# First mixer of a two-layer transformer step: VectorE's modulation sums from three tiles in the heads and four in the out-projection, tied to the attention's reciprocals, at other rates

## The chip, the cores and the metric

One core of one Trainium2 chip. The metric is the device time of one execution in microseconds (us). The instructions run on TensorE (PE: matmuls, with its weight loads PEld beside them), VectorE (DVE), ScalarE (ACT), GpSimd (POOL), and SyncE (SP), whose queue issues nearly all DMA transfers. Each engine runs its own list of instructions in a fixed order, and waits on semaphores for what others produce.

## The reference, cut to what matters

One inference step of a network of width D = 2048 with two layers, for 128 context tokens and 128 latent tokens. Each layer is a mixer (attention) and a gated feed-forward part with a convolution; each of these reads a normalized input that is shifted and scaled, and adds its output times a gate:

```python
mod = silu(cond) @ w_ada            # per layer 6 x 2048 numbers for each of the two groups
shift, scale, gate = ...            # of the mixer, and three more of the feed-forward part
h = rmsnorm(x, g) * (1 + scale) + shift
x = x + gate * mixer(h)             # layer 0: MLA and GQA heads, one in- and one out-projection
h = rmsnorm(x, g2) * (1 + scale2) + shift2
x = x + gate2 * ffn(h)              # layer 1 the same with differential attention
```

The matrix `w_ada` is read once, and each of its blocks of 128 x 2048 numbers gives only two columns of `mod`: it is memory traffic with little arithmetic. All of it is float32.

## The kernel before, in words

The kernel holds the activations in SBUF with the features on the partitions: a tile is 128 features by 256 tokens (128 context, 128 latent). A product of a weight block and an activation is made of three TensorE matmuls on numbers split in two: weight high times activation high (`wh`, `hx`), `wh` times the activation's low part, and weight low (`wl`) times the high part. A weight tile `raw` of 1 MB comes by DMA (line 284); ScalarE casts it to `wh` and VectorE subtracts to get `wl` (line 258 and 259, in pieces of 128 x 1024, or 128 x 512 where `fine[0]` is set). TensorE's order within a stage is: the gemms of the stage one after the other (16 blocks of 128 x 128 each, 48 matmuls of 128 x 256).

The stages of the first layer, by the profile's times: the in-projection to some 200 us, the attention heads to 316 us (`mixer_ab`, loop over `h`), the out-projection to 421 us (`out_ab`, loop over `c`, sixteen output blocks, each with its residual sum `x` on line 878), then the normalization of the feed-forward's input and the feed-forward itself.

`w_ada` for the later parts is worked off beside these stages in two ways:

- On TensorE: `row_step` loads a tile `araw` of 1 MB (line 615, two buffers), multiplies it with the condition (`ada<-araw,condw`, in pairs of tiles), ScalarE copies the sums (`am`, line 447), and TensorE transposes them (line 113) for VectorE to add up (lines 455 to 464). `pump(rate)` after a gemm gives so many steps of it; what is left over of a unit lies in the list `later`.
- On VectorE: class `Deep`. A tile of 512 KB (`block`, `kvb` or `more`, line 553) is multiplied with the condition of the two groups and summed along its rows, two instructions of 128 x 1024 (line 543, each with a short read of the accumulator). `deep.rate` says how many such sums a pump issues; `deep.tiles` names the homes that the tiles take turns in, `deep.junk` the scratch that the products go to; with `deep.ahead` the next tile is loaded when one is begun. `settle()` at `h == 6` finishes what was loaded in the heads, `flush()` in the out-projection issues all the steps that are left. In the first layer it has 64 sums in all.

The order on each engine is that of a scheduler in the framework, which is free to move instructions by its own costs, except those given to `keep_order`, which stay in program order among themselves. VectorE's modulation sums and their loads are so pinned; TensorE's instructions are when `pe.in_turn` is set. SP's queue is one list too: a load that waits for its buffer holds up those behind it.

The out-projection begins with `first_three`, which runs blocks c = 0 to 2 together, since the last heads come late; from c = 3 on it is one gemm after the other. A gemm there begins with the second half of its weight tile (`first=8`).

Of the kernel before, what the change touches and what calls it, by code (L numbers as in the profile page):

```python
# [18 lines left out]
P = 128  # L19
D = 2048  # L20
KD = D // P
T = 128
NT = 2 * T
# [33 lines left out]
QUIET = [4, 3, 3]  # L57
# [28 lines left out]
RLIMIT = {"ab": 16, "ffn0": 17, "c": 22, "ffn1": 22}  # L86
FLIMIT = {"ab": 0, "ffn0": 12, "c": 12, "ffn1": 16}

SIDE = {"in3": 0.5, "heads": 1.9, "out0": 1.85, "c": 2.2, "outc": 2.0}
UW = NT + 2  # L90
INV = {2048: 0, 768: 1, 512: 2, 128: 3, 256: 4}

# [2 lines left out]
def step_kernel(ctx: ExitStack, tc: tile.TileContext, A: dict):  # L95
# [298 lines left out]
    pinned = [False]  # L394
    done = set()
    later = []

    class HalfUnit:

# [38 lines left out]
    def ada_finish(l, j, q):  # L438

        got = {}  # L440

        def home():
            return T_(ppool["ada"], [P, 512], "ada", bufs=1)

        def copy():
            got["am"] = T_(tmp, [P, 512], "am", bufs=1)
            (keep_order if pe.in_turn else lambda i: i)(act.copy(got["am"], ada["ps"]))

        def turn(pin=None):
            pt = bank() if pin else home()  # L450
            pin = pin or (lambda i: i)
            for b in range(4):
                pin(pe.transpose(pt[:, b * P:(b + 1) * P], got["am"][:, b * P:(b + 1) * P], ident))
            out = mod[:, l, j, 4 * q:4 * q + 4]
            dve.tensor_reduce(out=out, in_=pt.rearrange("p (b g r) -> p b r g", b=4, g=4)[:, :, 0:2],
                              axis=AX.X, op=ALU.add)
            dve.tensor_tensor(out=out, in0=out, in1=vector("bada", l, j, q), op=ALU.add)
            scales(l, j, q, out)

        return [copy, turn]  # L460
# [43 lines left out]
    class Deep:  # L504
# [30 lines left out]
        def sums(self, half, i, u, t, c):  # L535
            if c == 0:
                if not self.got:
                    self.load()
                self.raw = self.got.pop(0)
            self.mid = c == 0  # L540
            l, j, q = u
            out = self.part[:, i, t, c:c + 1] if half else mod[:, l, j, 4 * q + t, c:c + 1]
            keep_order(dve.tensor_tensor_reduce(  # L543
                out=self.junk, in0=self.raw, in1=self.row[:, c].rearrange("p (g n) -> p g n", g=2),
                scale=1.0, scalar=0.0, op0=ALU.mult, op1=ALU.add, accum_out=out))
            if c == 0 and self.ahead and self.loads:
                self.load()

        def load(self):
# [53 lines left out]
    feed = Feed()  # L603

    def row_step(until=len(ROWS)):
        if later:
            later.pop(0)()
        if ada["i"] >= until:
            return
        l, j, q = ROWS[ada["i"]]  # L610
        t, g = divmod(ada["t"], 4)

        def load(t):
            ada["raw"] = T_(wpool, [P, 4, 512], "araw", bufs=2)
            sp.dma_start(out=ada["raw"], in_=A["w_ada"][l, j, q, t])
            return ada["raw"]

        def sum_pair(t, pair):
            for i in (1, 0):
                sum_rows(t + i, pair[i], (1, 0, 3, 2))  # L620

        if pinned[0]:
            if (t, g) == (2, 0):
                sum_pair(0, ada["pair"])
            if t % 2 == 0 and g < 2:
                ada["pair"] = [load(t)] if g == 0 else ada["pair"] + [load(t + 1)]
            if (t, g) == (3, 3):
                last = ada["pair"]
                later.append(lambda: sum_pair(2, last))
        else:  # L630
            if g == 0:
                load(t)
            if g == 3:
                sum_rows(t, ada["raw"])
        ada["t"] += 1
        if ada["t"] == 16:
            later.extend(ada_finish(l, j, q))
            ada["i"] += 1
            ada["t"] = 0

    def pump(rows, feats=0.0, until=None, beside=True):

        until = until or RLIMIT[stage[0]]
        step()
        if beside:
            deep.pump()
# [290 lines left out]
    def head_ab(pl, s, rs, v, hx, c):  # L937
# [3 lines left out]
        p = T_(pl, [P, 3 * T], "p", bufs=3)  # L941
        softmax_parts(s, mx, sums, rs, None, p)
        rec = T_(small, [P, 2], "rec")
        dve.reciprocal(out=rec, in_=sums)
        yield
        act.activation(p[:, :T], p[:, :T], AF.Identity, scale=rec[:, 0:1])
        act.activation(p[:, T:], p[:, T:], AF.Identity, scale=rec[:, 1:2])
# [10 lines left out]
    def mixer_ab(hx, beside):  # L958
        l = 0
        with tc.tile_pool(name="ab", bufs=1) as ab:  # L960
# [307 lines left out]
            with tc.tile_pool(name="abh", bufs=1) as hp:  # L1268
# [62 lines left out]
                accs[:] = [0, 1]  # L1331
                start(gqa_query(0))
                deep.copies = []
                deep.tiles.append((ab, "kvb"))
                deep.junk = o[:, 6:8]
                deep.rate, deep.ahead = SIDE["heads"], True
                for h in range(0, 8, 2):
                    if h == 4:
                        deep.junk = qb[:, 0:4].rearrange("p c n -> p (c n)").rearrange("p (g n) -> p g n", g=2)
                    for i in range(2):  # L1340
                        ps = gemm(WQ.chunk(), qh, qlo)
                        qn[h + i] = T_(hp, [P, NT], "qn", bufs=4)
                        act.copy(qn[h + i], ps)
                        pump(RATE["heads"])
                    ps = gemm(WQ.chunk(), qh, qlo)
                    ev = T_(tmp, [P, NT], "nt", bufs=4)
                    act.copy(ev, ps)
                    qr = T_(hp, [P, NT], "qr", bufs=2)
                    act.copy(qr[:, 0:T], ev[:, 0:T])
                    rope(qr[:, None, T:], ev[:, None, T:], 1, 32, "rcm", "rsm")  # L1350
                    pump(RATE["heads"])
# [17 lines left out]
    def out_ab(o, st, u, beside, rp):  # L1369
# [3 lines left out]
        ada["pew"] = PEW["out0"]  # L1373
        W = Weights(A["w_out_ab"], KD, 1)
        oh, ol = (lambda k: o[:, k, :NT]), (lambda k: o[:, k, NT:2 * NT])
        deep.tiles = [(beside, "block"), (rp, "more")]
        deep.junk = u[:, 14:16, :512]
        turn["acc"] = 0
        ready = first_three(W, oh, ol, PAIR_LATE, first=1, third=lambda: att_bank(0))
        for c in range(KD):  # L1380
            fine[0] = c in (3, 4) or c >= KD - QUIET[1]
            add = gated if 3 <= c < KD - QUIET[1] else residual
            add(ready.pop(0) if ready else gemm(W.chunk(), oh, ol, first=8), l, 0, c, st)
# [3 lines left out]
                deep.flush()  # L1387
                deep.ahead = False
            rows(c)
            pump(RATE["out0"] if c < KD - QUIET[1] else 0)  # L1390


    nlam = T_(keep, [P, 1], "nlam")
# [449 lines left out]
```

## Time and profile before

| | before |
|---|---|
| time, median of 3 runs | 2291.29 us (2291.23 to 2292.58) |
| the profiled execution's own time | 2291.7 us |
| its span, first to last instruction | 2289.9 us |
| granted TensorE clock | 0.998 |
| TensorE busy | 2267.4 us (99%) |
| VectorE busy | 1880.3 us (82%) |
| ScalarE busy | 1211.6 us (53%) |
| loads from memory | 609.32 MB, 268 GB/s over the span |

A line of the timeline has the start in us, the time in us, engine, line of the kernel, operation, output and inputs by the program's names, shapes, and in brackets how long the engine stood idle before it and what ended that. A line of the table of stretches has the stretch, its length, and for PE, PEld, DVE, ACT and POOL the busy time with the count of instructions, then TensorE's granted clock, the DMA engines' busy share and the rate in GB/s. The profiled execution's time is 1.8 us more than its span.

### The profile page before, as it was taken

Reading aid. Unit: us, or ns where it says so; the run is one execution under the profiler, and the core shown is the slowest. Engines: PE = TensorE matmul, PEld = TensorE weight load, DVE = VectorE, ACT = ScalarE, POOL = GpSimd, SP = SyncE. Lnnn points to the kernel's source line nnn. Section 1 sums busy time; section 2 is a strip of 40 time slices with the busy share of each in tenths; the row PEclk is TensorE's granted clock in tenths of the full one; section 3 lists DMA queues with packets and bytes.
Section 4 is the critical chain, followed back from the end, with each engine's and each line's share of the span. In section 5 each row is a group of like instructions: output and inputs, shape, how many; then the busy total and the mean of one; then the engine's idle time right before and its main releaser. Section 6 shows DMA issues by size and latency. Waiting matters only on the chain.

```text
span 2289.9 us, 47508 instructions
## 1 busy us (share of the span) xinstructions
PE 2267.4 (99%) x19496; PEld 2178.6 (95%) x19496; DVE 1880.3 (82%) x2975; ACT 1211.6 (53%) x2045; POOL 185.5 (8%) x216
## 2 busy tenths in 40 slices
PE   9999999999999999999999999999999999999998
PEld 6788888999999999999999999999999999999998
DVE  4768879889989999999978988898899955666654
ACT  4446666765553455555575455457555434555543
POOL 0011004300000000001130000023000000000011
PEclk9999999999999999999999999999999999999999
DMA  9998989767768777677778888776677655555553
GB/s 395 371 354 290 344 325 358 304 249 275 255 245 310 294 259 275 248 268 268 284 290 301 319 312 311 264 269 227 249 267 256 254 199 200 188 200 187 202 187 127
DMA packets 100121, 617.14 MB, mean 270 GB/s; under 512 B 10752, under 2 KB 18880, under 8 KB 33344
## 3 DMA queue, kind: packets, MB, share of 16 engines
q1 hardware_dynamic: 99904, 614.11, 72.4%
q8 instruction: 153, 2.51, 0.4%
q14 instruction: 64, 0.52, 0.1%
HBM read 609.32 MB, written 4.75 MB: 268 GB/s over the span
## 4 chain that ended last, share of the span: by engine, by line
PE 77%; DVE 2%; DMA 1%; POOL 1%; issue 0%; ACT 0%; DVEq 0%; ACTq 0%
PE acc L110 75%; PE att L110 1%; PE ada L110 1%; DVE wl L259 1%; DMA more<-w_ada 0%; DVE hx L543 0%; DMA block<-w_ada 0%; POOL dev L842 0%; PE att L113 0%; DVE x L1700 0%; POOL hxc L846 0%; DVE rope L901 0%; DVE dev L834 0%; PE ada L113 0%; ACT p L917 0%
## 5 line engine op out<-in xcount | busy, mean ns | idle before, releaser
L110 PE MATMUL acc<-hx,wh 128*128 128x256 f32 (+1 forms) x7232 | 1248.1, 278 | 3.9 <-ACT wh L258 1.5
L258 ACT CAST wh<-raw 128x1024 fp32r<-128x1024 f32 (+1 forms) x870 | 798.8, 935 | 834.6 <-PE acc L110 699.7
L259 DVE TENSOR_TENSOR wl<-raw,wh 128x1024 fp32r<-128x1024 f32 (+1 forms) x870 | 930.5, 1087 | 235.8 <-ACT wh L258 228.2
L110 PEld LDWEIGHTS acc<-hx,wh 128*128 128x128 f32 x7232 | 1092.4, 188 | 24.4 <-issue 15.1
L110 PE MATMUL acc<-hx,wl 128*128 128x256 f32 (+1 forms) x3616 | 1003.0, 278 | 0.9 <-DVE wl L259 0.7
L110 PEld LDWEIGHTS acc<-hx,wl 128*128 128x128 f32 x3616 | 679.6, 188 | 4.3 <-issue 1.7
L110 PE MATMUL acc<-g,wh 128*128 128x256 f32 x2816 | 478.8, 277 | 0.0
L110 PEld LDWEIGHTS acc<-g,wh 128*128 128x128 f32 x2816 | 423.9, 188 | 0.0
L110 PE MATMUL acc<-g,wl 128*128 128x256 f32 x1408 | 388.8, 277 | 0.0
L483 DVE CUSTOM_DVE_ANT_0 junk<-araw,condb 128x2048 f32<-128x2048 f32 x128 | 294.3, 2299 | 0.0
L110 PEld LDWEIGHTS acc<-g,wl 128*128 128x128 f32 x1408 | 264.3, 188 | 0.0
L211 POOL TENSOR_TENSOR sqacc<-sqacc,sq 128x256 f32<-128x256 f32 x62 | 73.0, 1177 | 1472.8 <-ACT sq L207 1468.3
L110 PE MATMUL acc<-hxc,wh 128*128 128x256 f32 (+1 forms) x1056 | 189.2, 281 | 0.0
L110 PEld LDWEIGHTS acc<-hxc,wh 128*128 128x128 f32 x1056 | 162.0, 188 | 1.8 <-issue 1.7
L110 PE MATMUL acc<-hxc,wl 128*128 128x256 f32 (+1 forms) x528 | 147.1, 279 | 0.0
L110 PEld LDWEIGHTS acc<-hxc,wl 128*128 128x128 f32 x528 | 99.6, 189 | 0.2
L110 PE MATMUL acc<-wh,hxc 128*128 128x256 f32 (+1 forms) x512 | 95.0, 283 | 0.8 <-DVE nt L853 0.8
L1593 ACT ACTIVATE cv<-acc,convw 128x256 f32<-128x256 f32 x169 | 94.2, 558 | 0.0
L1599 DVE SCALAR_TENSOR_TENSOR cv<-acc,convw,cv 128x254 f32<-128x254 f32 x169 | 81.0, 479 | 3.2
L110 PEld LDWEIGHTS acc<-wh,hxc 128*128 128x128 f32 x512 | 79.5, 188 | 3.7 <-issue 2.5
L1596 DVE SCALAR_TENSOR_TENSOR cv<-acc,convw,cv 128x254 f32<-128x254 f32 x169 | 80.4, 476 | 0.0
L543 DVE CUSTOM_DVE_ANT_0 hx<-block,condb 128x1024 fp32r<-128x1024 f32 x60 | 73.1, 1219 | 4.4 <-DMA block<-w_ada 4.3
(291 smaller groups left out, 1804.1 us busy)
## 6 DMA issues: line engine op xcount, KB each, us to landing
raw<-w_up SPq DMA_DIRECT2D x176, 1024.0 KB, 4.8
araw<-w_ada SPq DMA_DIRECT2D x132, 1024.0 KB, 6.1
raw<-w_down SPq DMA_DIRECT2D x88, 1024.0 KB, 4.8
raw<-w_in_c SPq DMA_DIRECT2D x48, 1024.0 KB, 6.4
block<-w_ada SPq DMA_DIRECT2D x42, 512.0 KB, 6.7
raw<-w_in_ab SPq DMA_DIRECT2D x18, 1024.0 KB, 9.5
raw<-w_out_ab SPq DMA_DIRECT2D x16, 1024.0 KB, 6.8
raw<-w_out_c SPq DMA_DIRECT2D x16, 1024.0 KB, 5.6
```

Of the source, the lines that this page charges most:

```text
L110: return self.placed(nc.tensor.matmul(*a, **kw))
L211: eng.tensor_tensor(out=st["acc"], in0=st["acc"], in1=sq, op=ALU.add)
L258: pin(act.copy(out_hi, src))
L259: pin(dve.tensor_tensor(out=out_lo, in0=src, in1=out_hi.bitcast(F32), op=ALU.subtract))
L483: keep_order(dve.tensor_tensor_reduce(out=T_(feat["pool"], [P, D], "junk"), in1=feat["row"][:, c], in0=feat["raw"].rearrange("p g n -> p ( ...
L543: keep_order(dve.tensor_tensor_reduce(out=self.junk, in0=self.raw, in1=self.row[:, c].rearrange("p (g n) -> p g n", g=2), scale=1.0, scala ...
L1593: pin(act.activation(y, ps, AF.Identity, scale=cw[:, 1, m:m + 1], bias=cw[:, 3, m:m + 1]))
L1596: pin(dve.scalar_tensor_tensor(out=y3[:, :, 1:], in0=p3[:, :, :T - 1], scalar=cw[:, 0, m:m + 1], in1=y3[:, :, 1:], op0=ALU.mult, op1=ALU.add))
L1599: pin(dve.scalar_tensor_tensor(out=y3[:, :, :T - 1], in0=p3[:, :, 1:], scalar=cw[:, 2, m:m + 1], in1=y3[:, :, :T - 1], op0=ALU.mult, op1=A ...
```

## The change

It alters how many modulation sums VectorE does in which stage of the first mixer, from how many tiles, and how TensorE's share of the same work is put between the gemms of the out-projection:

- In the heads a pump issues 2.2 sums, not 1.9, from three homes (`block`, `kvb`, `block` of the head pool) instead of two; room for the third comes from fewer buffers of `qn` and `qr`. In the out-projection it issues 1.4, not 1.85, from four homes instead of two.
- A tile begun in `Deep.sums` now loads ahead until one home less than all is filled.
- The reciprocal of the softmax sums is pinned among the VectorE sums.
- In the out-projection, c = 3 to 11, TensorE runs in program order; the steps on TensorE come at a rate of 0 for c < 4 and 0.9 after, instead of 0.62 throughout, and after the ScalarE copy of a unit the transposes wait for the next pump (`hold`). The last also holds in the heads of the second mixer.

```diff
-SIDE = {"in3": 0.5, "heads": 1.9, "out0": 1.85, "c": 2.2, "outc": 2.0}
+SIDE = {"in3": 0.5, "heads": 2.2, "out0": 1.4, "c": 2.2, "outc": 2.0}
...
+    hold = [False]
...
             (keep_order if pe.in_turn else lambda i: i)(act.copy(got["am"], ada["ps"]))
+            hold[0] = pe.in_turn
...
-            if c == 0 and self.ahead and self.loads:
+            while c == 0 and self.ahead and self.loads and len(self.got) < len(self.tiles) - 1:
                 self.load()
...
     def row_step(until=len(ROWS)):
-        if later:
+        if later and not hold[0]:
             later.pop(0)()
+            if pe.in_turn and len(later) == 2:
+                later.pop(0)()
...
         until = until or RLIMIT[stage[0]]
+        hold[0] = False
         step()
...
-        dve.reciprocal(out=rec, in_=sums)
+        keep_order(dve.reciprocal(out=rec, in_=sums))
...
-                deep.tiles.append((ab, "kvb"))
+                deep.tiles += [(ab, "kvb"), (hp, "block")]
...
-                        qn[h + i] = T_(hp, [P, NT], "qn", bufs=4)
+                        qn[h + i] = T_(hp, [P, NT], "qn", bufs=2)
...
-                    qr = T_(hp, [P, NT], "qr", bufs=2)
+                    qr = T_(hp, [P, NT], "qr", bufs=1)
...
-        deep.tiles = [(beside, "block"), (rp, "more")]
+        deep.tiles = [(beside, "block")] + [(rp, f"more{i}") for i in range(3)]
...
         for c in range(KD):
+            pe.in_turn = 3 <= c < KD - QUIET[1]
...
-            pump(RATE["out0"] if c < KD - QUIET[1] else 0)
+            pump(0 if c < 4 else 0.9 if c < KD - QUIET[1] else 0)
```

By the order of the instructions, 32 sums lie in the first half of the heads before and after; 16 before and 24 after go to the scratch `qb` (the heads' second half and the begin of the out-projection), and 16 before and 8 after to the scratch `u` (the rest of the out-projection).

VectorE's order at the begin of the out-projection, before: from the split of the last but one head's output (`hx`) to the weights of block c = 3 (`wl_4225` is the second half of its tile, with which its gemm begins; `x_76` is the residual sum of blocks 0 to 2; `ISA ... 128x1024` is a modulation sum, with the read of its accumulator behind it):

```order
L259 TENSOR_TENSOR wl_4219<-raw_4216,wh_4218 128x512 x2
L259 TENSOR_TENSOR hx_2451<-acc_723_3917,hx_2451 128x256
L543 ISA qb_241,mod_77<-kvb_3528,condb_3178 128x1024
L543 ISA mod_77 128x1
L543 ISA qb_241,mod_77<-block_3632,condb_3178 128x1024
L543 ISA mod_77 128x1
L455 TENSOR_REDUCE mod_77<-ada_3889 128x8
L543 ISA qb_241,mod_77<-block_3632,condb_3178 128x1024
L543 ISA mod_77 128x1
L457 TENSOR_TENSOR mod_77<-mod_77,cst_74 128x8
L464 SCALAR_TENSOR_TENSOR scl_78<-mod_77,cst_74 128x8
L878 SCALAR_TENSOR_TENSOR x_76<-acc_743_3987,mod_77,x_76 128x128 x2
```

The same place after (`wl_4234` is the second half of c = 3's tile there):

```order
L259 TENSOR_TENSOR wl_4228<-raw_4225,wh_4227 128x512 x2
L259 TENSOR_TENSOR hx_2451<-acc_727_3935,hx_2451 128x256
L566 TENSOR_TENSOR mod_77<-mod_77 128x8
L545 ISA qb_241,mod_77<-block_3544,condb_3108 128x1024
L545 ISA mod_77 128x1
L567 TENSOR_TENSOR mod_77<-mod_77,cst_74 128x8
L545 ISA qb_241,mod_77<-block_3544,condb_3108 128x1024
L545 ISA mod_77 128x1
L545 ISA qb_241,mod_77<-kvb_3567,condb_3108 128x1024
L545 ISA mod_77 128x1
L545 ISA qb_241,mod_77<-kvb_3567,condb_3108 128x1024
L545 ISA mod_77 128x1
```

Directly behind these stand the residual sums of c = 0 and c = 1, and only then the first piece of `wl_4234`; before, the residual of c = 0 is followed by the first piece of `wl_4225`. From the split of the head before (`hx_2451<-att_722_3916` before, `hx_2451<-att_726_3934` after) to the first residual there are four sums before and seven after.

SP's queue in the out-projection, before (`raw_4465` to `raw_4627` are the weights of c = 6 to 8, `araw` TensorE's tiles, `more` and `block` VectorE's):

```order
L284 DMA raw_4465<-w_out_ab 128x2048
L284 DMA raw_4539<-w_out_ab 128x2048
L615 DMA araw_4187<-w_ada 128x2048
L615 DMA araw_4189<-w_ada 128x2048
L284 DMA raw_4627<-w_out_ab 128x2048
L553 DMA more_4211<-w_ada 128x1024
L553 DMA block_4214<-w_ada 128x1024
```

and after, from the weights of c = 6:

```order
L284 DMA raw_4460<-w_out_ab 128x2048
L284 DMA raw_4545<-w_out_ab 128x2048
L284 DMA raw_4625<-w_out_ab 128x2048
L555 DMA more_765_4216<-w_ada 128x1024
L555 DMA more_766_4219<-w_ada 128x1024
L555 DMA more_767_4221<-w_ada 128x1024
L555 DMA block_4223<-w_ada 128x1024
L619 DMA araw_4385<-w_ada 128x2048
L619 DMA araw_4387<-w_ada 128x2048
```

The pair of `araw` that stood ahead of c = 8's weights now stands behind them and behind four tiles of VectorE's, and no tile for VectorE is loaded in the out-projection after these four until the next stage's.

TensorE's order at the end of c = 6's gemm, before (the transposes of line 113 inside the gemm; its pair of `ada<-araw` stands earlier in the same gemm):

```order
L110 MATMUL acc_801_4475<-hx_2451,wh_4467 128x256
L113 MATMUL ada_4386<-cst_74,am_4382 128x128 x4
L110 MATMUL acc_801_4475<-hx_2451,wh_4467 128x256
L110 MATMUL acc_801_4475<-hx_2451,wl_4468 128x256
L110 MATMUL acc_801_4475<-hx_2451,wh_4467 128x256 x2
L110 MATMUL acc_801_4475<-hx_2451,wl_4468 128x256
L110 MATMUL acc_810_4549<-hx_2451,wh_4545 128x256 x2
```

and after:

```order
L110 MATMUL acc_801_4470<-hx_2451,wl_4463 128x256
L110 MATMUL acc_801_4470<-hx_2451,wh_4462 128x256 x2
L110 MATMUL acc_801_4470<-hx_2451,wl_4463 128x256
L110 MATMUL ada_4376<-araw_4387,condw_79 32x512 x4
L110 MATMUL ada_4376<-araw_4385,condw_79 32x512 x4
L110 MATMUL acc_812_4555<-hx_2451,wh_4551 128x256 x2
```

The pair's sums moved to the gap between the gemms of c = 6 and c = 7, the transposes to the next gap; from c = 4 to c = 11 nothing stands inside a gemm any more. The number of matmuls is the same.

## The prediction

> **What bounds the kernel now.** I read the page's busy shares first, then the table of stretches through the two stages that change, then who TensorE waited for, and last the timeline at the places that the order of the instructions points to.
>
> ```profile
> span 2289.9 us, 47508 instructions
> PE 2267.4 (99%) x19496; PEld 2178.6 (95%) x19496; DVE 1880.3 (82%) x2975; ACT 1211.6 (53%) x2045; POOL 185.5 (8%) x216
> ```
>
> TensorE is the bound: of 2289.9 us it is not busy in 22.5. The change leaves its matmuls as they are, so it can win only idle time or pace, and it can lose wherever TensorE is made to wait. The stretches from the last heads to the end of the out-projection (after the stretch: its length, PE, PEld, DVE, ACT, POOL, clock, DMA share, GB/s):
>
> ```profile
> 300.00:320.00 20.00, 20.00 (x153) 15.88 (x151) 14.47 (x44) 16.26 (x38) 1.37 (x2) 1.00 0.81 310
> 320.00:340.00 20.00, 20.00 (x173) 18.09 (x170) 14.21 (x32) 8.13 (x20) 0.00 (x0) 1.00 0.98 381
> 340.00:360.00 20.00, 20.00 (x175) 18.43 (x174) 19.83 (x36) 13.12 (x30) 7.34 (x6) 1.00 1.02 401
> 360.00:380.00 20.00, 20.00 (x175) 18.04 (x177) 16.77 (x27) 12.78 (x27) 8.49 (x7) 1.00 0.94 353
> 380.00:400.00 20.00, 20.00 (x175) 17.58 (x167) 18.43 (x28) 11.35 (x27) 7.85 (x7) 1.00 0.87 331
> 400.00:420.00 20.00, 20.00 (x177) 19.68 (x174) 18.12 (x37) 11.79 (x27) 5.46 (x5) 1.00 0.87 322
> ```
>
> TensorE is busy in all of it. VectorE has 5.5 and 5.8 us to spare in the first two stretches and 0.17 in the third, where the DMA engines are full too (401 GB/s). From 200 to 440 us the table of TensorE's waits has one line:
>
> ```profile
> PE att L110 <- ACT sq L207: 0.6, 1, 0.6
> ```
>
> So in the changed stages there is hardly a wait to remove. What the profile of after can show is mainly new waits.
>
> **The change part by part.**
>
> *More sums in the heads (2.2, three tiles).* Eight sums move from the out-projection into the second half of the heads. VectorE has room, but not everywhere. The critical place is c = 3, the first gemm after the three joint blocks. VectorE's timeline from the split of the last but one head on:
>
> ```profile
> 328.00 0.42 DVE L259 TENSOR_TENSOR hx<-att,hx 128x256 fp32r<-128x256 f32 x1 [3.87 <-ACT hx L258]
> 328.52 1.90 DVE L259 TENSOR_TENSOR wl<-raw,wh 128x512 fp32r<-128x512 f32 x3
> 330.85 1.23 DVE L543 CUSTOM_DVE_ANT_0 qb<-kvb,condb 128x1024 f32<-128x1024 f32 x1 [0.43 <-DMA kvb<-w_ada]
> 332.00 1.89 DVE L259 TENSOR_TENSOR wl<-raw,wh 128x512 fp32r<-128x512 f32 x3
> 333.81 0.42 DVE L259 TENSOR_TENSOR hx<-acc,hx 128x256 fp32r<-128x256 f32 x1
> ...
> 335.41 1.23 DVE L543 CUSTOM_DVE_ANT_0 qb<-block,condb 128x1024 f32<-128x1024 f32 x1
> ...
> 336.68 1.23 DVE L543 CUSTOM_DVE_ANT_0 qb<-block,condb 128x1024 f32<-128x1024 f32 x1
> ...
> 339.44 0.61 DVE L878 SCALAR_TENSOR_TENSOR x<-acc,mod,x 128x128 f32<-128x128 f32 x2 [1.24 <-PE acc L110]
> 339.98 0.69 DVE L259 TENSOR_TENSOR wl<-raw,wh 128x512 fp32r<-128x512 f32 x1
> ```
>
> The last row is the first piece of the weights that c = 3 begins with; it is done at 339.98 + 0.69 = 340.67. TensorE takes it at once:
>
> ```profile
> 340.60 0.39 PE L110 MATMUL acc<-hx,wh 128*128 128x256 f32 x2
> 340.82 0.29 PE L110 MATMUL acc<-hx,wl 128*128 128x256 f32 x1
> ```
>
> The slack is 0.15 us. In the new order seven sums stand between this `hx` and the residual, not four, and the residual sums of c = 0 and c = 1 both stand ahead of the weights. The `hx` itself can't come earlier, since ScalarE sets it free at 328.00 and one sum more ahead of it takes only 1.27 (336.68 less 335.41) of its 3.87 us of idle time. So the piece comes later by 3 x 1.27 + 0.54 (a pair of residuals, 339.98 less 339.44) less the idle 0.43 and 1.24 that are filled: 2.68 us, at 343.35, and TensorE, which has its order fixed and nothing else to take, stands still for 343.35 - 340.82 = 2.5 us. The lower end is 0.4: were VectorE at its residual in time as before, the second residual pair alone would cost 0.54 less the slack of 0.15. The upper end is 3.0, if a tile's landing holds it by 0.43 again. I take **+2.5**, since each of its pieces is a row. Behind it stand, on VectorE, c = 4's weights; TensorE's delay moves their due time by as much, so nothing is added.
>
> *Reciprocals pinned.* The last GQA head's reciprocal moves behind the two maxima of the last MLA pair's first head on VectorE. These rows are VectorE's (the reciprocal, and the first of the maxima) and ScalarE's:
>
> ```profile
> 313.02 0.16 DVE L944 RECIPROCAL rec<-sums 128x2 f32<-128x2 f32 x1
> ...
> 315.74 0.29 DVE L910 TENSOR_REDUCE mx<-att 128x1 f32<-128x128 f32 x1 [1.36 <-PE acc L110]
> ```
> ```profile
> 317.77 0.48 ACT L926 COPY pT<-misc 128x384 f32<-128x384 f32 x1 [0.43 <-PE misc L113]
> ```
>
> It would come at 316.3 or later (315.74 and two maxima of 0.29 each or more), 3.3 us later, and the transposes that ScalarE's row copies follow its scaling by ScalarE. TensorE has gemms to run meanwhile, if their order puts them there. Between 0 (hidden) and 3.3 (nothing in between); I take **0**, as the table of waits has no softmax in the heads for which TensorE waits. The reduced `qn` and `qr` buffers go with this: their writers on ScalarE are ahead of TensorE, 0.
>
> *Out-projection: TensorE's pairs between gemms, tiles in one bunch.* On SP's queue the weights of c = 8 and four tiles (1 MB and 4 x 0.5 MB) now go ahead of a pair of `araw` (2 MB). These are SP's and TensorE's rows of before:
>
> ```profile
> 352.31 0.33 SPq L284 DMA_DIRECT2D raw<-w_out_ab  x1
> 354.04 0.33 SPq L553 DMA_DIRECT2D more<-w_ada  x1
> ```
> ```profile
> 361.31 1.92 PE L110 MATMUL ada<-araw,condw 128*32 128x512 f32 x16
> 363.17 0.50 PE L110 MATMUL acc<-hx,wh 128*128 128x256 f32 x2
> ...
> 366.22 0.60 PE L113 MATMUL ada<-cst,am 128*128 128x128 f32 x4
> 366.57 0.37 PE L110 MATMUL acc<-hx,wh 128*128 128x256 f32 x1
> ...
> 367.24 0.39 PE L110 MATMUL acc<-hx,wh 128*128 128x256 f32 x2
> ```
>
> The last row begins c = 7. Without the pair (363.17 less 361.31) and the transposes (0.35) inside c = 6 it would begin at 365.0, with the wait at c = 3 at 367.5, and there the pair is due. The weights' load is issued when VectorE is through with c = 5, at some 353 (352.31 before). 5.24 MB at 401 GB/s take 13.1 us and end at 366.1; at 322, the slowest stretch above, 16.3 us, at 369.3. So the pair is late by 0 to 1.8 us, and so is the next one behind the weights of c = 11: 0 to 3.6 in all. I take **+0.6**, nearer to the stretch of 401, since there the queue was full as it will be here. [...]
>
> The 1.86 and 0.35 us that the pair and the transposes cost inside a gemm they cost between gemms as well. What a gemm loses by being broken off no row shows apart; I bound it by one matmul's step, 20/177 = 0.11 us, at each of six places, to either side (-0.7 to +0.7), and take **-0.3**, since between gemms the target changes anyhow.
>
> *Out-projection without late sums.* The one wait in the table above comes from here. VectorE's and ScalarE's rows:
>
> ```profile
> 421.94 1.22 DVE L543 CUSTOM_DVE_ANT_0 u<-block,condb 128x1024 fp32r<-128x1024 f32 x1
> ```
> ```profile
> 423.20 0.99 ACT L734 ACTIVATE u<-x,scl 128x128 fp32r<-128x128 f32 x3 [0.56 <-DVE mod L543]
> 424.09 0.40 ACT L207 ACTIVATE sq<-x 128x256 f32<-128x256 f32 x1
> ```
>
> Sums stand between the last residuals and hold the last `x`, and so ScalarE's squares. The new order has no sum there, and 1.2 us less is more than the 0.6 that TensorE waited: **-0.6** (-0.6 to 0). What is late next there is TensorE itself.
>
> *Second mixer (`hold`).* A row of transposes moves by one pump, some sums shift. Its waits on TensorE, from 1150 to 1560 us:
>
> ```profile
> PE acc L110 <- DVE nt L853: 0.8, 1, 0.8
> PE acc L110 <- ACT hx L258: 0.3, 1, 0.3
> PE acc L110 <- ACT dv L1474: 0.2, 1, 0.2
> ```
>
> None is of the moved rows: **0**, between -1.3 (all three gone) and +1.3 (as much again).
>
> The sum is 2.5 + 0 + 0.6 - 0.3 - 0.6 + 0 = +2.2 us. It is made on the execution of 2291.7 (its span 2289.9 and 1.8 around it), which stands 0.4 above the median of 2291.29; against the median it gives **2293.5 us**. A measurement of this kernel can tell about 0.2%, 4.6 us, from no change, so this is no change.
>
> **The rivals.**
>
> *Hidden anyway.* The eight sums fall into VectorE's spare 11.3 us of the first two stretches, and the waits at c = 3 and for the pair don't come: only the 0.4 of the residual pair, and -0.6 and -0.3 on the other side, 2290.8. For it speaks the spare time; against it that 3.87 us of that lie before the `hx` that ScalarE releases.
>
> *Slower: the DMA queue.* TensorE in program order has nothing to put in front of a pair that isn't there. Place: the gaps ahead of c = 7 and c = 9. If the bunch of 5 MB lands at 322 GB/s and the pair after it is held by the weights of c = 11, each is late by 1.8 us, and a third by as much if the lateness goes on to the weights behind them in the queue: 2.2 - 0.6 + 5.4 = +7.0, 2298.3. It decides from 2.4 us on top of the sum, that is when the pairs come some 3 us late in all. For it: a full queue at 340 to 360 us; against: the load there ends when no tile follows.
>
> [...]
>
> *Faster: pace.* In the out-projection TensorE starts 173 to 177 matmuls in 20 us; were all at 177, the four stretches with fewer would save 2 + 2 + 2 + 4 = 10 matmuls of 20/177 us, 1.1 us. With the 0.6, the second mixer's 1.3 and no wait at all, that is -3.0, 2288.3, still no change by 4.6. More than that has no row to come from but the heads, whose pace can't be read from counts.
>
> **How the numbers follow.** My forecast 0.46; hidden anyway 0.22; the queue 0.17; the clock 0.03; pace 0.12, of which half for a gain in the heads that goes beyond 4.6 us. Slower takes the queue and most of the clock: 0.19; faster 0.06; the rest, 0.75, is no change. The range goes from the pace rival's 2288.3 to the queue rival's 2298.3 and leaves out less than 2 in 10: half of those two rivals, and what no row foretells.
>
> **What would show it.** A wait of TensorE for VectorE's `wl` at some 341 us, 2 to 3 us long, is the main term; if it isn't there, the second rival's first step fails too. Waits on `araw` by DMA at 365 to 382 us, if any, price the queue. The wait for `sq` at 424 should be gone. VectorE should be busier than 14.5 and 14.2 in the first two stretches, and idle longer from 400 on. I am wrong if TensorE's time changes without a wait in these tables, in the heads above all, or if a stretch outside of 200 to 440 us moves by over 1.5 us.

## The result, and the profile after

The changed kernel is slower: 2299.96 us (median of 6 runs, 2299.06 to 2301.16) against 2291.73 us before on the same chip (6 runs, 2291.23 to 2292.58). The ratio is 1.0035, 95% interval 1.0025 to 1.0045. I had forecast 2293.5, no change that can be told, and a range to 2298.3; the kernel lost 8.2 us, more than that range allows. Below, `+x us` is the median less that of the kernel before in the same set of runs. A trace is of one execution, which lies up to 1.9 us from its kernel's median.

The head of the page, and the stretches that the prediction showed, after the change:

```profile
span 2297.3 us, 47515 instructions
PE 2272.5 (99%) x19496; PEld 2181.2 (95%) x19496; DVE 1881.2 (82%) x2975; ACT 1212.3 (53%) x2045; POOL 184.6 (8%) x216
```
```profile
300.00:320.00 20.00, 20.00 (x147) 16.43 (x144) 18.36 (x51) 14.56 (x36) 1.37 (x2) 1.00 0.70 247
320.00:340.00 20.00, 20.00 (x176) 17.02 (x174) 16.42 (x34) 7.63 (x19) 0.00 (x0) 1.00 0.94 365
340.00:360.00 20.00, 18.76 (x159) 16.84 (x156) 19.32 (x42) 11.99 (x30) 6.51 (x5) 1.00 0.92 369
360.00:380.00 20.00, 16.01 (x119) 12.84 (x119) 18.08 (x24) 10.26 (x20) 6.54 (x5) 0.83 0.99 389
380.00:400.00 20.00, 20.00 (x175) 18.43 (x174) 13.39 (x22) 10.59 (x23) 6.00 (x6) 1.00 0.78 299
```

VectorE is busier in the first two stretches (18.36 and 16.42, before 14.47 and 14.21) and idle more after 380, as the change says. But TensorE, which was busy without a gap, now has one of 1.24 us and one of 3.99, and in 360 to 380 a mean clock of 0.83. Its waits from 200 to 440 us:

```profile
PE ada L110 <- DMA araw<-w_ada: 4.0, 1, 4.0
PE acc L110 <- DVE wl L259: 1.2, 1, 1.2
```

The first is the pair of `araw` ahead of c = 7. SP's queue in its order (start, time to the last issue of the group), and TensorE's row:

```profile
344.72 10.77 SPq L284 DMA_DIRECT2D raw<-w_out_ab  x3
356.34 2.14 SPq L555 DMA_DIRECT2D more<-w_ada  x3
358.52 0.51 SPq L555 DMA_DIRECT2D block<-w_ada  x1
359.13 1.16 SPq L619 DMA_DIRECT2D araw<-w_ada  x2
362.42 12.00 SPq L284 DMA_DIRECT2D raw<-w_out_ab  x3
```
```profile
371.94 3.64 PE L110 MATMUL ada<-araw,condw 128*32 128x512 f32 x16 [3.99 <-DMA araw<-w_ada]
375.51 0.80 PE L110 MATMUL acc<-hx,wh 128*128 128x256 f32 x2
```

The third `raw` of the first group (c = 8) was issued at 355.16, when VectorE was through with c = 5's `wl` (353.92 + 1.21 = 355.13). The four tiles of the bunch stand behind it and the pair behind those. The pair's two tiles were issued at 359.13 and 359.61 and landed at 369.42 and 371.90; the next weights came into the queue 2.8 us after them and shared it. The pair's matmuls take 3.64 us, not 1.92 as before. The same place by stretches (TensorE's clock is the third number from the end):

```profile
367.00:369.00 2.00, 0.96 (x9) 0.76 (x7) 2.00 (x5) 1.23 (x3) 0.00 (x0) 1.00 1.02 430
369.00:370.00 1.00, 0.00 (x0) 0.00 (x0) 1.00 (x3) 0.45 (x2) 0.47 (x1) 0.98 1.02 434
370.00:372.00 2.00, 0.06 (x4) 0.06 (x8) 2.00 (x2) 0.66 (x3) 1.47 (x2) 0.50 0.97 410
372.00:376.00 4.00, 4.00 (x18) 1.02 (x19) 4.00 (x8) 0.69 (x3) 0.97 (x1) 0.50 0.99 371
376.00:378.00 2.00, 2.00 (x16) 2.00 (x16) 1.97 (x3) 0.23 (x1) 0.00 (x0) 0.80 0.97 373
```

TensorE stopped at 367.95; at 369.96 (0.98 of the second row is a fall 0.04 us before its end) the clock went to half and came back at 376.8.

Where the time went, by the start of the first matmul at seven places (TensorE's timeline; between each two of them lie the same matmuls in both kernels, 1050, 160, 116, 112, 308 and 60):

| place | before | after | shift | new in this part |
|---|---|---|---|---|
| heads | 203.05 | 203.19 | +0.15 | |
| c = 3 | 340.60 | 341.90 | +1.30 | +1.15 |
| c = 6 | 359.18 | 362.31 | +3.13 | +1.83 |
| c = 8 | 372.68 | 382.20 | +9.52 | +6.39 |
| c = 10 | 385.77 | 395.45 | +9.68 | +0.16 |
| feed-forward, first block | 421.41 | 430.81 | +9.40 | -0.28 |
| feed-forward, second block | 429.54 | 437.89 | +8.35 | -1.05 |

From there to 1222 us the shift is 8.31 without a change. The profiled execution is 7.4 longer in all. The remaining 0.9 goes in the second mixer: 0.12 at 1348 us and 0.77 between 1460 and 1490; from 1500 us to the end the shift is 7.42.

### The profile page after: what moved, and what is told of

The parts are those of the page before. It is cut to its first block, busy times and chain, and to the rows that moved or that the text cites. A ratio compares the mean times of both kernels' runs of the same rounds, so it can differ in the third digit from the quotient of the medians.

```text
span 2297.3 us, 47515 instructions
## 1 busy us (share of the span) xinstructions
PE 2272.5 (99%) x19496; PEld 2181.2 (95%) x19496; DVE 1881.2 (82%) x2975; ACT 1212.3 (53%) x2045; POOL 184.6 (8%) x216
## 4 chain that ended last, share of the span: by engine, by line
PE 94%; DVE 2%; DMA 2%; ACT 1%; POOL 1%; issue 0%; SPq 0%; DVEq 0%; ACTq 0%
PE acc L110 88%; PE ada L110 3%; PE att L110 2%; DMA araw<-w_ada 1%; DVE qb L545 1%; DVE wl L259 1%; PE misc L110 0%; DMA kvb<-w_ada 0%; PE att L113 0%; POOL dev L847 0%; PE ada L113 0%; PE misc L113 0%; DVE x L1706 0%; POOL hxc L851 0%; DVE dev L839 0%
## 5 line engine op out<-in xcount | busy, mean ns | idle before, releaser
L545 DVE CUSTOM_DVE_ANT_0 hx<-block,condb 128x1024 fp32r<-128x1024 f32 x65 | 79.3, 1220 | 2.4 <-DMA block<-w_ada 2.2
```

Source lines behind the costliest of these rows:

```text
L545: keep_order(dve.tensor_tensor_reduce(out=self.junk, in0=self.raw, in1=self.row[:, c].rearrange("p (g n) -> p g n", g=2), scale=1.0, scala ...
```

## The experiments

Theory Q: four tiles for VectorE in one bunch, on one queue with TensorE's pairs and the weights, and the sums behind them, make something late for TensorE between c = 6 and c = 9. Theory D: TensorE's fixed order puts a pair where it can't be there yet. Theory K: the idle wait lets the clock fall. Rival H: the heads' part is the root of it all. A kernel is named by what it changes; "changed kernel" is the one of the result above.

**Two tiles in the out-projection** (from the changed kernel):

```diff
-        deep.tiles = [(beside, "block")] + [(rp, f"more{i}") for i in range(3)]
+        deep.tiles = [(beside, "block"), (rp, "more")]
```

> The changed kernel (2299.96 us) with only the out-projection's tiles put back: two homes (block, more) instead of four, so that 1 MB instead of 2 MB of VectorE's tiles stands on SP's queue ahead of the pair of araw for the gap before c = 7. Theory Q (the bunch on the queue is what makes that pair late): 1.05 MB less at 424 GB/s is 2.5 us; TensorE's wait of 3.99 us shrinks to some 1.5, the clock doesn't fall (that cost some 2.6), the time is about 2294.9. Rival L (the pair is late because its two buffers come free late, after the pair before it in the gap ahead of c = 5): the wait and the fall stay, 2299 to 2300. Rival H (the heads' eight more sums make all that follows late): 2299 to 2300 as well, the wait at c = 3 of 1.24 stays in either case.

Measured: 2301.07 us, +8.5 (1.0038, 1.0023 to 1.0053). The wait ahead of c = 7 did shrink, to 1.5 us, and the clock was 1.00 from 345 to 380 us. The two other tiles, though, now stand ahead of the next pair, and TensorE's fixed order waits for that one:

```profile
PE ada L110 <- DMA araw<-w_ada: 5.7, 2, 4.1
PE acc L110 <- DVE wl L259: 1.7, 1, 1.7
```
```profile
389.15 3.58 PE L110 MATMUL ada<-araw,condw 128*32 128x512 f32 x16 [4.15 <-DMA araw<-w_ada]
```

So Q's price for the first pair is right and its total (2294.9) wrong: with program order a smaller bunch only moves the wait.

**The heads' part undone** (1.9 sums, two tiles, the buffers and the free reciprocals of before; the out-projection as changed):

```diff
-SIDE = {"in3": 0.5, "heads": 2.2, "out0": 1.4, "c": 2.2, "outc": 2.0}
+SIDE = {"in3": 0.5, "heads": 1.9, "out0": 1.4, "c": 2.2, "outc": 2.0}
...
-                deep.tiles += [(ab, "kvb"), (hp, "block")]
+                deep.tiles.append((ab, "kvb"))
...
-        keep_order(dve.reciprocal(out=rec, in_=sums))
+        dve.reciprocal(out=rec, in_=sums)
```

> The changed kernel with its part in the heads taken back (1.9 sums a pump, two tiles, four qn and two qr buffers, the reciprocals not pinned); the out-projection stays as changed, so the eight sums come there at 1.4 a pump from four tiles. Theory Q: the bunch still stands ahead of araw, TensorE still waits 2 to 4 us for a pair and the clock falls; only the heads' own 1.15 and the wait of 1.24 for wl at c = 3 go: about 2297.5. Rival H (late sums are the root, they make c = 5's weights and so SP's queue late): the wait for araw goes too, 2291 to 2292.

Measured: 2297.09 us, +4.6 (1.0023, 1.0014 to 1.0033). The forecast of 2297.5 holds. The wait at c = 3 and the loss ahead of it are gone, the wait for the pair isn't:

```profile
368.71 3.26 PE L110 MATMUL ada<-araw,condw 128*32 128x512 f32 x16 [4.16 <-DMA araw<-w_ada]
```

A wait of 1.06 for the next pair comes on top. Rival H, as a root of everything, falls: the out-projection's part alone costs over half. And VectorE needn't be late from c = 3 on for the pair to be late: here the weights of c = 8 were issued at 349.36 already, but the first of the four tiles waited 2.1 us for a sum of VectorE, and the pair's second tile, behind the four, was issued at 357.05 and landed at 368.66.

**Filling the wait** (from the changed kernel; nothing reads the result of the 34 matmuls):

```diff
+    fill = []
...
         def sum_pair(t, pair):
+            if fill:
+                fill.pop(0)()
...
             pe.in_turn = 3 <= c < KD - QUIET[1]
+            if c == 5:
+                def filler():
+                    ps = att_bank(1)
+                    for n in range(34):
+                        pe.matmul(ps[:, :NT], o[:, 0, :P], oh(n % KD), start=(n == 0), stop=(n == 33))
+                fill.append(filler)
```

> The changed kernel with 34 matmuls of 128 x 256 that nothing uses put on TensorE right ahead of the pair of araw before c = 7, where it waits 3.99 us: 34 x 0.113 = 3.85 us of work that only fills the wait. The output is the same. Theory K (the idle wait lets the clock fall to half, which makes the pair 1.7 us and the next gemm some 0.9 us longer): the granted clock stays at 1.00 there and the time falls by 2.6 us to 2297.4, though there is more work. Rival (the pair and the gemm are slow for another reason, the memory traffic for one): no change, 2300.

Measured: 2299.57 us, +7.0 (1.0033, 1.0020 to 1.0046). The mechanism is as K says: the clock is 1.00 all through, and the pair takes 1.92 us again.

```profile
369.61 4.24 PE L110 MATMUL att<-hx 128*128 128x256 f32 x34
374.44 1.92 PE L110 MATMUL ada<-araw,condw 128*32 128x512 f32 x16 [0.60 <-DMA araw<-w_ada]
```
```profile
373.00:375.00 2.00, 1.40 (x16) 0.90 (x18) 2.00 (x3) 1.00 (x3) 1.28 (x2) 1.00 1.02 430
```

From the pair's start to c = 8 it saves 1.7 us in the pair and 0.8 in the gemm of c = 7. The forecast of the time missed, since the filler took 4.24 us and 0.60 of waiting stayed where there had been 3.99, another 0.6 came at the next pair, and the wait at c = 3 was 1.89 in this execution, not 1.24: 2.5 less 0.85, 0.6 and 0.65 leaves 0.4. Against the kernel before in its own set each, the two kernels' medians differ by 1.2 (8.2 and 7.0), with intervals that overlap: the times alone don't show the gain, the clock and the pair's duration do.

**The old rate for TensorE's pairs** (from the changed kernel):

```diff
-            pump(0 if c < 4 else 0.9 if c < KD - QUIET[1] else 0)
+            pump(RATE["out0"] if c < KD - QUIET[1] else 0)
```

> The changed kernel with TensorE's share of the sums at the old rate of 0.62 a gemm for c = 0 to 11 instead of 0 and then 0.9, still in program order between gemms. The pairs come a gap or two earlier, and on SP's queue one pair moves ahead of the bunch of four tiles. Theory L (the buffers of araw come free too late with the new rate): no wait ahead of c = 7, but a pair now stands right behind c = 3, where 2 us of waiting may come: 2293 to 2296. Theory Q by itself: the pair behind the bunch is due later (c = 8 or 9) and lands in time, 2293 to 2295. Rival H: 2299 to 2300.

Measured: 2304.06 us, +11.5 (1.0051, 1.0036 to 1.0066), the worst of all. In the fixed order only 1.9 us of other matmuls lie between the first pair, whose matmuls end at 339.87, and the second, which is due at 341.81. The second was issued at 339.81 and 340.29, as the first left the two buffers, and landed at 350.63:

```profile
350.76 3.64 PE L110 MATMUL ada<-araw,condw 128*32 128x512 f32 x16 [8.96 <-DMA araw<-w_ada]
```

I had expected 2 us, one gemm later. Here the bunch is behind the pair, so this wait is D's and not Q's: a pair needs its distance.

**Program order taken away, and pairs spread further** (each from the changed kernel):

```diff
-            pe.in_turn = 3 <= c < KD - QUIET[1]
```

> The changed kernel without the one line that puts TensorE in program order in the out-projection; SP's queue keeps the bunch ahead of the pair of araw, but the scheduler now puts that pair's sums one gemm and a half later, inside c = 8 instead of in the gap before c = 7. Theory D (the pair's place in TensorE's order is too early for a pair that waits on the queue): no wait for it, no fall of the clock, 4.0 + 2.5 us less than the changed kernel's 2299.96, about 2293.5. Theory Q (the bunch on the queue alone): the pair lands as late as before, some 372, and is used at some 376, no wait either. What tells them apart is the run old_pump, where the bunch was behind the pair and TensorE still waited 9 us: by D a place that leaves the pair 12 us or more from its issue has no wait, by Q none is needed. Rival H (the heads' part is the root): 2299 to 2300.

```diff
-            pump(0 if c < 4 else 0.9 if c < KD - QUIET[1] else 0)
+            pump(0 if c < 4 else 0.62 if c < KD - QUIET[1] else 0)
```

> The changed kernel with TensorE's share of the sums at 0.62 a gemm from c = 4 on, not 0.9; program order, the bunch and the heads as changed. The first pair stays in the gap before c = 5, the second moves from the gap before c = 7 to the one before c = 8, 5.5 us later, with the same loads ahead of it on SP's queue. Theory D: 5.5 us are more than the 4.0 that were missing; no wait, no fall of the clock, 2293.5. Theory Q taken alone says the queue is what it was, so the pair would land as late as it did; it forecasts no wait there as well, but a wait for the next pair if the queue is the bound: 2294 to 2297. Rival H: 2299 to 2300.

Measured: 2298.46 us, +6.7 (1.0026, 1.0015 to 1.0037) and 2299.07 us, +7.3 (1.0032, 1.0020 to 1.0043). No wait for a pair in either, as D says, and still hardly a gain: TensorE now waits for `wl` of c = 9, one row for each kernel.

```profile
384.92 0.39 PE L110 MATMUL acc<-hx,wl 128*128 128x256 f32 x1 [1.96 <-DVE wl L259]
```
```profile
384.04 0.58 PE L110 MATMUL acc<-hx,wl 128*128 128x256 f32 x1 [2.60 <-DVE wl L259]
```

On VectorE (the kernel without program order) the piece stands behind the bunch's sums, though its `raw` had landed at 375.7:

```profile
376.67 1.22 DVE L545 CUSTOM_DVE_ANT_0 u<-more,condb 128x1024 fp32r<-128x1024 f32 x1
...
377.93 1.64 DVE L545 CUSTOM_DVE_ANT_0 u<-more,condb 128x1024 fp32r<-128x1024 f32 x1
...
380.02 1.21 DVE L545 CUSTOM_DVE_ANT_0 u<-block,condb 128x1024 fp32r<-128x1024 f32 x1
...
381.28 1.23 DVE L545 CUSTOM_DVE_ANT_0 u<-block,condb 128x1024 fp32r<-128x1024 f32 x1
...
382.43 1.22 DVE L259 TENSOR_TENSOR wl<-raw,wh 128x1024 fp32r<-128x1024 f32 x1
```

The clock fell to 0.50 behind these waits too, for 3.42 and 3.40 us. The forecasts of 2293.5 missed; the wait found another place. The slower of the two times is the one that rival H gave (2299 to 2300), but not for its reason alone, since the heads' own part costs 2.4, as the next run shows.

**The heads' part alone** (on the kernel before: the edits of "heads undone" the other way round, and the loop in `Deep.sums`):

> The kernel before (2291.7 us) with the heads' part of the change alone: 2.2 sums a pump from three tiles, qn and qr with fewer buffers, the reciprocals pinned, and the loading ahead in Deep.sums; the out-projection as before at 1.85. By the table of the changed kernel the heads cost 1.15 us before c = 3 and a wait of 1.24 for wl at c = 3 with 0.4 behind it; its late sums in the out-projection become fewer, but flush still puts some at the end. Theory: +2.8, at most -1.0 for the statistics: 2293.5 to 2294.5. Rival (the waits of the changed kernel come from the out-projection's part alone): 2291.7.

Measured: 2294.15 us, +2.4 (1.0013, 1.0003 to 1.0022), as expected, with a wait of 1.4 for `wl` at c = 3.

**Heads' part and program order both undone:**

> The changed kernel without its part in the heads and without program order in the out-projection: what is left are four tiles at 1.4 sums a pump there, the rates of 0 and 0.9, and hold. Theory D with the heads' part priced at 2.75 us: both costs are gone, nothing waits, and the statistics' wait of 0.6 is gone as in the changed kernel: 2290.5 to 2292. Rival (four tiles in a bunch cost by their traffic): 2294 to 2297 with waits for araw.

Measured: 2293.03 us, +1.3 (1.0005, 0.9996 to 1.0015), no difference that can be told, though 1 us above the range. The statistics' wait is 0.41 here, not gone, and two of 0.53 and 0.35 stand behind it. Four tiles in a bunch cost nothing that these runs can tell where VectorE isn't late and TensorE's order is free. So rival H is right in part: without program order the heads' part makes 5.4 us of difference (+6.7 and +1.3), more than its own 2.4.

**No transfers for the bunch** (from the changed kernel; it leaves out the loads, and the sums read the last tile again):

```diff
             half, u, t = self.loads.pop(0)
+            if len(self.tiles) == 4:
+                self.got.append(self.raw)
+                return
```

> The changed kernel without the transfers of VectorE's tiles in the out-projection: the sums there read the last tile again, so part of the modulation is wrong; every instruction on VectorE, ScalarE and TensorE stays, and SP's queue lacks the four tiles of 2 MB ahead of the pair. Theory Q: the pair is issued at some 357 instead of 359, with 3 MB instead of 5 MB on the way, lands at 363 to 365, and TensorE waits neither for it nor, with a late weight tile, for wl; no fall of the clock: 4.0 + 2.5 us less, 2293.5, with the wait at c = 3 of 1.2 to 1.9 still there. Rival V (VectorE's late sums, not the traffic, make the weights of c = 5 and all that follows late): the wait ahead of c = 7 stays at 2 us or more and the time at 2297 or above.

Measured: 2297.80 us, +5.5 (1.0023, 1.0014 to 1.0032). The wait for the pair and the fall of the clock are gone (1.00 in every stretch from 340 to 430 us), though the weights of c = 8 were as late as in the changed kernel (357.20, with c = 3 begun 1.5 us later): the pair was issued at 357.69 and 358.55 and landed at 368.06, while TensorE, without the wait below, would have come for it at 370.0. So the bunch on the queue was their cause. But the sums, no longer held by their tiles, come earlier on VectorE and hold c = 6's weights:

```profile
366.64 0.39 PE L110 MATMUL acc<-hx,wl 128*128 128x256 f32 x1 [2.07 <-DVE wl L259]
```

Half of each theory: Q is right on the pair, V on what comes in its place. The order that the scheduler gives moved with the edit, so the two are not cleanly apart.

**Heads' part without the pinned reciprocals, and three tiles alone** (both on the kernel before):

> The kernel heads_only (2294.15 us: the kernel before with the heads' part of the change) without the pinned reciprocals. Theory: the order of VectorE at c = 3 is the same (seven sums between the last but one head's split and the residual), so the wait for wl of 1.4 stays; the 1 us lost ahead of c = 3 comes from the score matmuls that the later reciprocals break up, and it goes: 2293. Rival: the loss ahead of c = 3 comes from the extra sums and smaller buffers; no change, 2294.

> The kernel before with three tiles in the heads and the loading ahead alone, at the old rates, reciprocals free, out-projection as before. Two sums less come late, and five, not four or seven, stand between the last but one head's split and the residual of c = 0. One sum more is 1.27 us, and 1.67 us of idle time are there: theory C (the wait at c = 3 comes from how many sums stand there) forecasts at most 0.5 us of waiting at c = 3 and a time of 2291 to 2292.5. Rival: three tiles cost by their loads or by the smaller qn and qr, 2293.5 or more, with a loss ahead of c = 3 as in heads_only.

Measured: 2294.69 us, +2.4 (1.0012, 1.0003 to 1.0021): c = 3 begins 1.7 us later than before, counted from the heads' start, so the loss ahead of it isn't the reciprocals'; my theory fell, and the wait was 2.40 (in an execution 1.9 us above the median). Three tiles alone: 2293.02 us, +0.7 (1.0002, 0.9993 to 1.0011), 0.5 above the range, with no wait of TensorE at all from 200 to 440 us. Five sums ahead of c = 3's weights fit into the idle time, seven don't; theory C holds. The rival has a part in it too: c = 3 begins 0.65 us later than before, counted the same way, with four transposes less ahead of it.

**What the bunch and the new rates do without program order** (both from the kernel without it; two homes for the tiles, or 0.62 for the pairs):

> The kernel no_turn (2298.46 us: the changed kernel without program order in the out-projection) with two homes for VectorE's tiles there instead of four. In no_turn TensorE waited 1.96 us for c = 9's wl at 383 us, whose raw landed at 375.7 and whose wl stood on VectorE behind six sums of the bunch. Theory Q (the bunch of four tiles delays that raw by traffic and its wl by the sums behind it): neither, the wait at c = 9 is gone, about 2294.5 as in heads_only. Rival R (the pairs that come later by the new rates use the queue at the wrong time): the wait for c = 9 or a neighbour stays, 2297 to 2299.

> The kernel no_turn with the old rate of 0.62 for TensorE's share of the sums, c = 0 to 11; four tiles in a bunch stay. One pair of araw goes ahead of the bunch on SP's queue. Theory Q (the bunch is the cost): a wait for wl of 1.5 to 2.5 us between c = 7 and c = 10 stays, 2297 to 2299. Rival R (the new rates are the cost): no such wait, 2294 to 2295, what the heads' part alone costs.

Measured: 2295.19 us, +2.7 (1.0010, 1.0000 to 1.0019), with no wait but the heads' at c = 3 and one of 0.5; and 2297.37 us, +4.9 (1.0022, 1.0012 to 1.0032). From 346 to 440 us, of the second:

```profile
PE acc L110 <- DVE wl L259: 1.1, 1, 1.1
PE acc L110 <- ACT wh L258: 0.8, 1, 0.8
```

With two homes what is left is about the heads' 2.4 us; with four there is a wait at either rate of the pairs, and rival R falls. No version of these is faster than the kernel before.

## Why the prediction was wrong, point by point

- *The wait at c = 3, +2.5.* Right in place and cause, half in size: 1.24 us, and 1.2 to 2.4 in the other kernels with the heads' part where this wait comes. I had the weights' piece at 343.35; it came at 343.57 (342.89 + 0.68). But TensorE itself came 1.3 us later, which I had not in the sum. One step was wrong and did no harm: it was not ScalarE's release of `hx` at 328.00 that held VectorE, but a late tile:

```profile
327.83 1.23 DVE L545 CUSTOM_DVE_ANT_0 qb<-kvb,condb 128x1024 f32<-128x1024 f32 x1 [3.51 <-DMA kvb<-w_ada]
```

- *The heads themselves, 0.* Wrong: 1.15 us are lost ahead of c = 3 without a wait that a table shows. I put all of it on the reciprocals and called it hidden; they make no difference. The matmuls' steps, start to start, tell where 1.03 of it lies: in the 64-row score matmuls that read `qr`. Before, four of them start within 0.01 us of the same matmul of another head, and the two run together; after, every one stands alone (the first four rows are of before, the last two of after):

```profile
315.01 0.48 PE L110 MATMUL att<-kr,qr 64*128 64x256 f32 x1
315.01 0.48 PE L110 MATMUL acc<-kr,qr 64*128 64x256 f32 x1
315.33 0.38 PE L110 MATMUL att<-kr,qr 64*128 64x256 f32 x1
315.33 0.38 PE L110 MATMUL acc<-kr,qr 64*128 64x256 f32 x1
...
312.46 0.70 PE L110 MATMUL att<-kr,qr 64*128 64x256 f32 x2
316.68 0.70 PE L110 MATMUL acc<-kr,qr 64*128 64x256 f32 x2
```

  The same 1.03 is lost in every kernel with three tiles and the smaller `qn` and `qr`, with the old rate and free reciprocals too, and in none with the old buffers. That the one buffer of `qr`, which I had put at 0, keeps the two heads apart is the likely reason; no run has it alone.
- *The pair ahead of c = 7, +0.6 for all pairs.* This is the step that failed. It was 3.99 us of waiting, and 2.4 of slow clock behind it. The mechanism, bytes ahead of the pair on SP's queue, was right; its size was wrong. I took the weights' issue at 353, the pair right behind it, and 13.1 us for 5.24 MB, at most 16.3; measured were 355.16 for the weights and 16.7 us from there to the pair's landing at 371.90. Over my upper bound of 1.8 us that is 2.2 for the later issue and 0.4 for the transfer, less 0.5, since TensorE stopped at 367.95 and not at 367.5. The queue was neither full from the start nor the pair's alone: SP had stood 5.4 us at the weights' buffer, which VectorE's `wl` frees, and so the DMA engines ran nearly dry (the last number is GB/s),

```profile
355.00:357.00 2.00, 2.00 (x18) 0.56 (x19) 1.93 (x5) 1.32 (x5) 1.15 (x1) 1.00 0.45 107
```

  the first of the tiles waited 0.8 us more for a sum of VectorE, the issues of the four took until 359.04, and the next weights shared the queue. From 355.16 to 371.90 it moved 5.98 MB, 357 GB/s on average. VectorE's lateness from c = 3, which I had written off ("nothing is added"), makes the weights' load of c = 8 2.8 us later than before, but it isn't what decides: with it and without the bunch the pair was in time, and with the bunch and without it TensorE waited 4.16.
- *The clock.* I gave it 0.03. In the trace of before it is 1.00 from 20 to 2270 us, and no row there shows a wait of TensorE with a slower clock behind it. After, it fell to 0.50 at c = 7 and cost 2.4 against the kernel before; the filler took back 2.5, 1.7 in the pair and 0.8 in the gemm behind it.
- *Queue as a rival, 2298.3, "each late by 1.8".* The right mechanism and place, with 0.17. It came as one wait of 3.99, not as three of 1.8, and its price lacked the clock.
- *No late sums, -0.6.* Right and somewhat more: the wait for the squares is gone, and the part shortened by 1.05 us.
- *Broken-off gemms, -0.3.* From c = 10 to the feed-forward 0.28 us are won, as taken; what of it is the order isn't separated. From c = 3 to c = 6 the same 160 matmuls lose 0.59 in their steps, beside the wait, and the cause of that stays open.
- *Second mixer, 0.* Within its range: TensorE's waits there are 0.8 and 0.3 as before, and the one of 0.2 is gone. The shift falls by 0.12 and 0.77. The 0.12 comes in most kernels with `hold` and in none without it; a gain of 0.4 to 0.7 at the place of the 0.77 also comes in the kernels that leave this stage as it was, so it can't be put down to the change.
- *The bandwidth.* This trace shows 430 and 434 GB/s in stretches where the DMA engines' share is 1.02 (367 to 370 us), above the 401 that I took. What I mis-sized was not this rate, but how full the queue would be and when the transfers began.

The sum as measured, place by place: 0.15 + 1.15 + 1.83 (of it 1.24 the wait) + 6.39 (3.99 the wait and 2.4 the clock) + 0.16 - 0.28 - 1.05 = 8.35.

## What to carry to other kernels

Where one queue feeds two engines, a load that is moved is to be followed to its issue time: what each load ahead of it waits for (a buffer, and the engine that frees it), and not only how many bytes are ahead, or at what rate. A fixed order turned the late loads here into idle time of the bound engine, and undoing one of the causes mostly moved the wait, so they have to be undone together. Idle time on TensorE is to be priced with the slow clock that came behind it here: 3.4 us at 0.50 behind single waits of 1.96, 2.40 and 2.60 us, and behind two of 0.80 and 1.09 close together. And a buffer that is taken away can cost overlap without a wait in any table, as here likely the 1.03 us ahead of c = 3: the steps of the matmuls show it.

## What the runs showed of the hardware

TensorE's granted clock fell to 0.50 behind some of its waits and stayed at 1.00 behind others. Of the single waits in these runs those of 1.24, 1.43, 1.70, 1.89 and 2.07 us left it at 1.00; 1.96, 2.40, 2.60, 3.99, 4.15, 4.16 and 8.96 brought it to half. So at about 2 us both happen. Two short waits had a fall behind them as well: in the last run (the old rate for the pairs, no program order) two waits close together, with two matmuls between them, were followed by 3.4 us at half clock, a mean of 0.83 over 380 to 390. In TensorE's rows of that run, by start and duration, with the wait in brackets:

```profile
382.04 0.39 PE L110 MATMUL acc<-hx,wh 128*128 128x256 f32 x2
383.23 0.50 PE L110 MATMUL acc<-hx,wh 128*128 128x256 f32 x2 [0.80 <-ACT wh L258]
384.81 0.58 PE L110 MATMUL acc<-hx,wl 128*128 128x256 f32 x1 [1.09 <-DVE wl L259]
```

They come to 1.89 us together; the fall came at 384.68, 0.13 before the second ended. After the single waits the fall came 2.0 to 4.1 us after the last matmul, and once (1.96) only after TensorE ran again. With 0.5 as the one lower value, the clock was at half for 3.40 to 3.42 us behind the waits of 1.96, 2.40, 2.60, 4.15 and 4.16; the rows of the kernel with pairs spread further give 383.54 to 386.94,

```profile
383.00:384.00 1.00, 0.00 (x0) 0.00 (x0) 1.00 (x3) 0.00 (x0) 0.00 (x0) 0.77 0.28 115
384.00:386.00 2.00, 1.96 (x9) 1.96 (x10) 2.00 (x5) 1.67 (x4) 0.16 (x1) 0.50 0.50 102
386.00:387.00 1.00, 1.00 (x7) 1.00 (x7) 1.00 (x2) 0.00 (x0) 1.00 (x1) 0.53 0.97 410
```

the changed kernel 369.96 to 376.8, and behind the wait of 8.96 it was 10.2 us. What decided between 1.96 and 2.07 us, no run was made to show.
